# Two of the four blocks of a mixer's v by seven products of quarters

## The chip, the cores and the metric

The kernel runs on one core of a Trainium2 chip. The metric is the device time of one execution in microseconds (us). The median of three timed runs of the kernel before is 1301.42 us (1301.41 to 1302.15). The profile is one more execution, of 1302.33 us by its own time, with a span of 1300.6 us from the first to the last instruction. The engines are named as in the profile: PE multiplies matrices, PEld loads its weights, DVE and ACT work on whole tiles, POOL does a few small things and issues some transfers, and SP issues most transfers.

## The reference

The model is a trunk of two layers over 512 tokens of width 1024, in float32. The first layer mixes tokens with a gated MLP; the change is in the product that makes this mixer's `z`, and of that in the half `v` (columns 2048 to 4095 of `w_in`).

```python
h = rms_norm(x, norm_mix[0])            # x * rsqrt(mean(x*x) + EPS) * gain
z = gelu(h @ w_in)                      # w_in: 1024 x 4096
u, v = split(z, 2, axis=-1)             # 512 x 2048 each
v = rms_norm(v, v_gain)
sv = einsum("gts,bcsgd->bctgd", tril(w_s), v in chunks of 128 tokens) + b_s
x = x + (u * sv) @ w_out
```

A gated convolutional MLP, a recurrent mixer, another gated MLP and a final norm follow, and are not touched.

## The kernel before, in words

Every float32 factor is split in two parts in PE's reduced format: `hi` is the rounded value (an ACT copy), `lo` the rest (a DVE subtraction). A product is three matmuls: hi by hi, lo by hi, hi by lo.

The product for `v` is made in four blocks of 512 columns (`fb`, 0 to 3). In a block each of the four groups of 128 tokens (`c`) has one PSUM bank of its own, `pss[c]`, 128 x 512; there are eight banks in all (pool `pp`). The 1024 rows of the weight are loaded in four steps (`kc`) of two slices of 128. A step is two slices by four groups by three, 24 matmuls of 512 columns: the parts of x are the stationary operand, the parts of the weight the moving one. Block 0 also loads and splits x (`first_chunk`); after it `norm_stat` adds up the squares and POOL raises the mean to the power -0.5. The result `rc` (L222, one factor for each token) scales the product of every block on its way through gelu: `v_gelu`'s two ACT instructions (L382 and L385 before, L446 and L449 after) read a bank, write `vr`, square it and leave the sum in `vsum`. After the last block the sums give a second factor `rv`, and `vh` and `vl` (L395 and L396, after L520 and L521) are the parts of the normed v.

Then come the four blocks of `u`, where x moves and the weight is stationary. Their result has the tokens along the free axis, so the factor `rc` must be spread over the partitions: `norm_spread` builds two diagonal tiles `dg` on DVE (L238), multiplies them by ones on PE (L242, bank `rb`) and copies the bank to `rbc` on ACT (L243).

In the later MLPs the down projection is done by `seven` and `weight_sums` (L469 to L479 and L518): four quarter products of a 2 x 2 arrangement are replaced by seven products of sums of quarters, each with a bank of 128 x 2 x 256. One step of it is seven products by two halves by three, 42 matmuls of 256 columns. Its weights come by three SP transfers, and two sums of quarters are made on the way by a POOL transfer that adds to what lies in the tile (L471 before, L346 after).

The pool `wp` has three buffers for each of the tags raw, hi and lo; `wk` has six work tiles in the mixer. A scheduler orders the instructions of each engine when the program is built, and that order is then fixed.

## Time and profile before

| what | value |
|---|---|
| median of three runs | 1301.42 us (1301.41 to 1302.15) |
| profiled execution, own time | 1302.33 us |
| its span | 1300.6 us |
| PE busy | 1290.2 us, 99% of the span |
| DVE busy | 933.9 us, 72% |
| ACT busy | 602.0 us, 46% |
| POOL busy | 54.3 us, 4% |
| PE's share of the chain that ended last | 92% |

A duration in a row is that of one instruction from start to end; instructions of one engine overlap a little, so the pace of a row of them is read from their starts. Times in rows count from the span's start. The `v` blocks run from 5.66 to 94.70 us, `u` from there.

### The profile page before, as it was taken

The numbers are of one execution on the slowest core, as the hardware profiler recorded it, in microseconds if no ns is written. First come the engines' busy times: TensorE is split into PE (matmuls) and PEld (weight loads), VectorE is DVE, ScalarE is ACT, GpSimd is POOL, SyncE is SP. The second block draws the span as 40 slices with busy tenths as digits, with TensorE's granted clock in tenths as the row PEclk, the third lists the DMA queues.
The fourth block names the chain that finished last, engine by engine and source line by source line (L and its number), as shares of the span: only waits on it lengthen the run. The fifth ranks groups of instructions, "written<-read, shape, count | busy, mean of one in ns | idle before, by whom it ended". The sixth has DMA issues, their size and how long they took to land.

```text
span 1300.6 us, 17029 instructions
## 1 busy us (share of the span) xinstructions
PE 1290.2 (99%) x6510; PEld 1100.3 (85%) x6510; DVE 933.9 (72%) x1336; ACT 602.0 (46%) x809; POOL 54.3 (4%) x56
## 2 busy tenths in 40 slices
PE   9999999999999999999999999999999999999997
PEld 7888888888888998888998888888888899888886
DVE  7227775446877887878997799954687788576734
ACT  6456332333444543445554679633344444343432
POOL 1000000000000120001200000000000011000000
PEclk9999999999999999999999999999999999999998
DMA  6333222233233574235753323233223357332221
GB/s 235 98 97 113 82 81 82 97 97 98 97 98 105 125 184 137 94 98 122 171 150 98 98 81 97 98 114 97 85 95 98 112 141 184 114 97 98 98 81 65
DMA packets 121105, 143.47 MB, mean 110 GB/s; under 512 B 7616, under 2 KB 95168, under 8 KB 121024
## 3 DMA queue, kind: packets, MB, share of 16 engines
q1 hardware_dynamic: 111088, 132.95, 32.3%
q0 software_dynamic: 9792, 9.44, 4.9%
q8 instruction: 51, 0.84, 0.3%
q14 instruction: 30, 0.25, 0.1%
q10 hardware_dynamic: 144, 0.00, 0.0%
HBM read 140.26 MB, written 2.10 MB: 109 GB/s over the span
## 4 chain that ended last, share of the span: by engine, by line
PE 92%; DVE 3%; DMA 2%; issue 1%; ACT 0%; DVEq 0%; SPq 0%; POOLq 0%; POOL 0%
PE f L112 12%; PE f L111 12%; PE f L113 12%; PE d061m L518 2%; PE d101m L518 2%; PE d001m L518 2%; PE d100m L518 2%; PE v L370 2%; PE u L111 2%; PE aop L111 2%; PE u L112 2%; PE v L372 2%; PE aop L112 2%; PE v L371 2%; PE u L113 2%; PE aop L113 2%
## 5 line engine op out<-in xcount | busy, mean ns | idle before, releaser
L454 DVE SCALAR_TENSOR_TENSOR cv<-up,vt,cv 128x511 f32<-128x511 f32 x192 | 135.7, 744 | 0.7
L541 DVE TENSOR_TENSOR up<-f,rbc 128x512 f32<-128x512 f32 x96 | 63.6, 686 | 31.7 <-PE f L113 30.2
L452 ACT ACTIVATE cv<-up,vt 128x512 f32<-128x512 f32 x96 | 70.7, 804 | 0.8 <-DVE up L541 0.8
L557 ACT ACTIVATE cv<-cv 128x512 f32<-128x512 f32 x48 | 30.4, 633 | 38.5 <-DVE cv L454 38.4
L498 DVE TENSOR_TENSOR y<-yr,y 128x1792 fp32r<-128x1792 f32 x18 | 36.5, 2026 | 13.7 <-ACT y L497 13.7
L497 ACT CAST y<-yr 128x1792 fp32r<-128x1792 f32 x18 | 30.6, 1698 | 15.0 <-DVE yr L495 14.5
L222 POOL TENSOR_TENSOR rc<-ms,mhalf 128x4 f32<-128x4 f32 (+1 forms) x6 | 5.5, 911 | 651.0 <-DVE ms L221 651.0
L430 DVE SCALAR_TENSOR_TENSOR sv<-sv,vt,bs 128x256 f32<-128x256 f32 x32 | 14.9, 477 | 16.4 <-PE sv L427 16.4
L207 ACT ACTIVATE xh<-xall,vt 128x512 fp32r<-128x512 f32 x24 | 17.1, 718 | 20.3 <-DVE xall L259 15.8
L216 ACT ACTIVATE sq<-xall 128x512 f32<-128x512 f32 (+1 forms) x37 | 21.5, 586 | 9.8 <-DVE xall L271 9.8
L559 DVE TENSOR_TENSOR yr<-cv 128x512 f32<-128x512 f32 x36 | 24.6, 687 | 1.7
L454 DVE SCALAR_TENSOR_TENSOR xb<-xr,vt,xb 128x511 f32<-128x511 f32 (+2 forms) x36 | 25.5, 744 | 0.2 <-ACT xb L452 0.2
L217 DVE TENSOR_TENSOR acc<-acc,sq 128x512 f32<-128x512 f32 (+1 forms) x37 | 23.7, 641 | 2.0 <-ACT sq L216 1.9
L208 DVE SCALAR_TENSOR_TENSOR xl<-xall,vt,xh 128x512 fp32r<-128x512 f32 x24 | 17.8, 746 | 3.4 <-ACT xh L207 3.2
L426 PE MATMUL sv<-ws,vh 128*128 128x256 f32 x64 | 15.4, 325 | 0.0
L432 DVE SCALAR_TENSOR_TENSOR sv<-sv,vt 128x256 f32<-128x256 f32 x32 | 15.0, 479 | 0.4
L563 ACT CAST y<-cv 128x512 fp32r<-128x512 f32 x12 | 7.3, 619 | 16.4 <-DVE cv L561 16.4
L427 PE MATMUL sv<-ws,vl 128*128 128x128 f32 x64 | 14.2, 222 | 0.0
L694 DVE TENSOR_TENSOR_SCAN hs<-riyh,sq 128x512 f32<-128x512 f32 x12 | 14.0, 1203 | 0.0
L86 ACT ACT_TABLE_LOAD x10 | 12.8, 1283 | 0.1
L493 DVE TENSOR_TENSOR yr<-yr 128x512 f32<-128x512 f32 x18 | 12.4, 691 | 0.6
L445 ACT ACTIVATE u<-u 128x512 f32<-128x512 f32 x16 | 9.3, 624 | 7.1 <-DVE u L444 7.1
(2631 smaller groups left out, 4477.2 us busy)
## 6 DMA issues: line engine op xcount, KB each, us to landing
xall<-xT SPq DMA_DIRECT2D x8, 256.0 KB, 5.1
outT<-o SPq DMA_DIRECT2D x8, 256.0 KB, 2.1
av00raw<-a_w_in SPq DMA_DIRECT2D x2, 256.0 KB, 3.8
av01raw<-a_w_in SPq DMA_DIRECT2D x2, 256.0 KB, 5.2
av02raw<-a_w_in SPq DMA_DIRECT2D x2, 256.0 KB, 5.6
av03raw<-a_w_in SPq DMA_DIRECT2D x2, 256.0 KB, 4.9
bs<-a_b_s SPq DMA_DIRECT2D x1, 512.0 KB, 5.8
av10r<-a_w_in SPq DMA_DIRECT2D x1, 512.0 KB, 6.0
```

Source lines behind the costliest of these rows:

```text
L111: nc.tensor.matmul(ps, wh, xh, start=first, stop=False)
L112: nc.tensor.matmul(ps, wh, xl, start=False, stop=False)
L113: nc.tensor.matmul(ps, wl, xh, start=False, stop=last)
L370: nc.tensor.matmul(pss[c], xh[kk][:, ts], hi[:, k, :], start=kk == 0, stop=False)
L371: nc.tensor.matmul(pss[c], xh[kk][:, ts], lo[:, k, :], start=False, stop=False)
L452: nc.scalar.activation(dst, src, AF.Identity, scale=col(wname, woff + last * wstep), bias=col(cname, coff))
L454: nc.vector.scalar_tensor_tensor(dst[:, i:], src[:, :S - i], col(wname, woff + (last - i) * wstep), dst[:, i:], op0=ALU.mult, op1=ALU.add)
L497: nc.scalar.copy(hi, raw[:, 0:7])
L498: nc.vector.tensor_tensor(lo, raw[:, 0:7], hi.bitcast(F32), op=ALU.subtract)
L518: nc.tensor.matmul(banks[b][:, j], wt[:, w, js], xt, start=first and j == 0 and m == 0, stop=last and j == 1 and m == 2, skip_group_check= ...
L541: nc.vector.tensor_tensor(upt, pss[2 * half + j], rbc, op=ALU.mult)
L557: nc.scalar.activation(ts[0], ts[0], AF.Gelu_apprx_tanh)
```

## The change

Blocks 0 and 1 of `v` stay as they are. Blocks 2 and 3 are computed by the seven products that the down projections use. The four quarters of the left factor are two slices of x (k) by two halves of the tokens (t); those of the right one are the two slices of the weight by two halves of the block's columns. The sums of quarters of x are made once, in the four steps of block 1 (`v_sums`: for each step two scaled copies on ACT, four subtractions or additions of 256 elements on DVE, and the split of two tiles, two ACT copies and two DVE subtractions). The sums of the weight are made in each step of blocks 2 and 3 by `weight_sums`. A block of this kind holds seven banks, and at its end ACT and DVE combine the seven banks to the four tiles `vr`, on which `v_gelu` then works in place.

`norm_spread` is moved from block 1 of `v` to the first block of `u`, behind its second step. The work pool has five tiles in place of six, and the sixth tile's room is the pool `sm` of `weight_sums`.

```diff
-    mixer = enter(("yp", 24), ("wk", 6), ("bs", 1))
+    mixer = enter(("yp", 24), ("sm", 1), ("wk", 5), ("bs", 1))
...
+    def v_sums(q):
+        g = []
+        for k in (2 * q, 2 * q + 1):
+            t = work(f"xg{k}")
+            nc.scalar.activation(t, xs[k], AF.Copy, scale=g0[:, k:k + 1])
+            g.append((t[:, 0:HS], t[:, HS:S]))
+        (p_, q_), (r_, s_) = g
+        a, b = work(f"xa{q}"), work(f"xb{q}")
+        nc.vector.tensor_tensor(a[:, 0:HS], p_, q_, op=ALU.subtract)
+        nc.vector.tensor_tensor(a[:, HS:S], s_, q_, op=ALU.subtract)
+        nc.vector.tensor_tensor(b[:, 0:HS], a[:, 0:HS], s_, op=ALU.add)
+        nc.vector.tensor_tensor(b[:, HS:S], b[:, 0:HS], r_, op=ALU.subtract)
+        parts = [to_parts(t, f"xq{q}{i}") for i, t in enumerate((a, b))]
...
-    for fb in range(4):
+    for fb in range(2):
...
-            if fb == 1 and kc == 2:
-                norm_spread()
...
+            else:
+                v_sums(kc)
...
+    for fb in range(2, 4):
+        banks = seven_banks(f"v{fb}")
+        for q in range(KD // 2):
+            parts = weight_sums(wv4[:, 2 * q:2 * q + 2, fb], f"av{fb}{q}")
+            for b, part, w, i in PRODUCTS:
+                wh, wl = (t[:, w] for t in parts[part])
+                sh, sl = xsums[q][i]
+                for j in range(2):
+                    js = slice(j * P, (j + 1) * P)
+                    for n, (st, mv) in enumerate(((sh, wh), (sl, wh), (sh, wl))):
+                        nc.tensor.matmul(banks[b][:, j], st[:, js], mv, start=q == 0 and j == 0 and n == 0,
+                                         stop=q == KD // 2 - 1 and j == 1 and n == 2, skip_group_check=True)
...
+            nc.scalar.copy(e1, banks[1])
+            for j in range(2):
+                nc.vector.tensor_tensor(vraw[j, fb][:, n1], banks[2][:, j], e1[:, j], op=ALU.add)
+            nc.vector.tensor_tensor(u2, banks[6], e1, op=ALU.subtract)
+            nc.vector.tensor_tensor(u3, u2, banks[7], op=ALU.subtract)
+            for j in range(2):
+                nc.vector.tensor_tensor(vraw[j, fb][:, n0], u3[:, j], banks[4][:, j], op=ALU.subtract)
+            nc.scalar.copy(e5, banks[5])
+            nc.vector.tensor_tensor(u2, e5, u2, op=ALU.subtract)
+            for j in range(2):
+                nc.vector.tensor_tensor(vraw[2 + j, fb][:, n1], banks[3][:, j], u2[:, j], op=ALU.add)
+        for j in range(2):
+            nc.vector.tensor_tensor(vraw[2 + j, fb][:, n0], u3[:, j], e5[:, j], op=ALU.subtract)
+        for c in range(NC):
+            v_gelu(c, fb, vraw[c, fb])
...
-        pss = block(KD, loader_of(a_w_in, mb * 512, f"au{mb}"), xparts, f"u{mb}", spatial_hooks(mb - 1) if mb else {})
+        pss = block(KD, loader_of(a_w_in, mb * 512, f"au{mb}"), xparts, f"u{mb}", spatial_hooks(mb - 1) if mb else {1: [norm_spread]})
```

The products in their order are 1, 2, 4, 6, 7, 5, 3: the first three read the part tiles `a` of the weight (quarters), the other four the tiles `b` (sums).

The scheduler puts the instructions of the engines in a new order. POOL first, at the end of block 0 of `v`. Before, the power that gives `rc` stands alone between the power of `log_sigmoid` (`lu`) and the masks of `w_s` (`wsm`):

```order
L186 TENSOR_TENSOR lu<-lu,nabs 128x12 [waits DVE_49,Pool_49]
L222 TENSOR_TENSOR rc<-ms,mhalf 128x4 [waits DVE_49]
L405 AFFINE_SELECT wsm<-wsr 128x256 [waits DMAHW7_49,Activation_49]
L405 AFFINE_SELECT wsm<-wsr 128x256 [waits Activation_49] x3
L222 TENSOR_TENSOR rv<-ms,mhalf 128x4 [waits DVE_49]
```

Now, at the same place (DMAHW7 and DMAHW0 are the landings of the first two transfers of `av20r`, the raw weights of block 2's first step):

```order
L186 TENSOR_TENSOR lu<-lu,nabs 128x12 [waits DVE_49,Pool_49]
L346 DMA av20r<-a_w_in 128x2x256 [waits DMAHW4_49,DMAHW2_49,DMAHW7_49,DMAHW0_49,DVE_49]
L222 TENSOR_TENSOR rc<-ms,mhalf 128x4 [waits DVE_49]
L346 DMA av21r<-a_w_in 128x2x256 [waits DMAHW5_49,DMAHW3_49,DMAHW6_49,DMAHW2_49,DVE_49]
L346 DMA av22r<-a_w_in 128x2x256 [waits DMAHW6_49,DMAHW5_49,DVE_49]
```

The adding transfer for block 2 stands ahead of the power, and waits for two transfers that SP issues when `av11l` has freed their buffer.

ACT next, from the last split of block 1 to block 1's gelu (`v0` to `v3` are the banks of block 1, `vr01` the gelu of the first of them). Before:

```order
L99 CAST av13h_448<-av13r_446 128x1024 [waits DMAHW6_49,DVE_49,PE_49]
L99 CAST av20h_498<-av20r_496 128x1024 [waits DMAHW7_49,DVE_49,PE_49]
L243 COPY rbc_88<-rb_414 128x512 [waits PE_49]
L99 CAST av21h_528<-av21r_526 128x1024 [waits DMAHW0_49,DVE_49,PE_49]
L382 ACTIVATE vr01_476<-v0_342,rc_127 128x512 [waits PE_49]
```

Now twenty instructions stand between `av13h` and that gelu: eight scaled copies `xg`, eight splits `xq`, and four splits of weights. These are the last of them and what follows:

```order
L353 CAST av20bhi_576<-av20r_564 128x512 [waits DMASW0_49,PE_49]
L353 CAST av20bhi_576<-av20s_569 128x512
L429 ACTIVATE xg7_525<-xall_70,g0_90 128x512
L249 CAST xq30h_533<-xa3_527 128x512 [waits DVE_49]
L249 CAST xq31h_537<-xb3_528 128x512 [waits DVE_49]
L353 CAST av21ahi_630<-av21r_624 128x768 [waits DMAHW3_49,DMAHW4_49,DMAHW2_49,PE_49]
L446 ACTIVATE vr01_541<-v0_345,rc_130 128x512
L446 ACTIVATE vr11_545<-v1_346,rc_130 128x512
L353 CAST av21bhi_636<-av21r_624 128x512 [waits DMASW1_49,PE_49]
L353 CAST av21bhi_636<-av21s_629 128x512
L449 ACTIVATE junk_543,vsum_137<-vr01_541 128x512 [waits Activation_49]
L449 ACTIVATE junk_547,vsum_137<-vr11_545 128x512 [waits Activation_49]
```

Behind them comes the gelu of `v2` and then that of `v3`. On PE the fifth, sixth and seventh product of block 2's first step write to the banks of `v0`, `v1` and `v2`, and each waits for ACT; the first eight matmuls of the second step stand between the sixth and the seventh product.

DVE last, in the first block of `u`, around the two diagonal tiles (`rch`, `rcl` are the parts of `rc`). Before, both are built in block 1:

```order
L233 CAST rch<-rc 128x4 [waits Pool_49]
L234 TENSOR_TENSOR rcl<-rc,rch 128x4 [waits DVE_49]
L100 TENSOR_TENSOR av12l<-av12r,av12h 128x1024 [waits DMAHW5_49,Activation_49]
L238 TENSOR_TENSOR dg<-ident,rch 128x512
L238 TENSOR_TENSOR dg<-ident,rcl 128x512 [waits DVE_49]
```

Now:

```order
L514 TENSOR_REDUCE vtot_1117<-vsum_137 128x4 [waits Activation_49]
L238 TENSOR_TENSOR dg_1275<-ident_122,rch_132 128x512 [waits DVE_49]
L221 TENSOR_SCALAR ms_131<-vtot_1117 128x4 [waits DVE_49]
L521 SCALAR_TENSOR_TENSOR vl00_1123<-vr00_329,rv_1118,vh00_1122 128x512 [waits Activation_49]
L521 SCALAR_TENSOR_TENSOR vl10_1127<-vr10_333,rv_1118,vh10_1126 128x512 [waits Activation_49]
L521 SCALAR_TENSOR_TENSOR vl20_1131<-vr20_337,rv_1118,vh20_1130 128x512 [waits Activation_49]
L521 SCALAR_TENSOR_TENSOR vl30_1135<-vr30_341,rv_1118,vh30_1134 128x512 [waits Activation_49]
L238 TENSOR_TENSOR dg_1278<-ident_122,rcl_133 128x512 [waits PE_49]
```

The first diagonal stands behind the sum of all squares of v, the second also behind the first four `vl`. On PE the first of the two matmuls of `rb` stands behind 48 matmuls of `u`, the second eight matmuls later.

## Rows read from the trace of the kernel before

**Rows 1.** The page: busy time (share of the span) x instructions, by engine.

```profile
PE 1290.2 (99%) x6510; PEld 1100.3 (85%) x6510; DVE 933.9 (72%) x1336; ACT 602.0 (46%) x809; POOL 54.3 (4%) x56
```

**Rows 2.** Stretches: length, each engine's busy time (instructions), PE clock, DMA share, GB/s.

```profile
28.00:50.00 22.00, 22.00 (x102) 18.29 (x101) 7.29 (x15) 12.07 (x23) 1.01 (x1) 1.00 0.35 105
```

**Rows 3.** Timeline, PE: start, duration, instruction, count; first of block 1, `rb`, first of `u`.

```profile
28.74 0.49 PE L370 MATMUL v<-av10h,xh 128*128 128x512 f32 x1
...
39.77 0.64 PE L242 MATMUL rb<-dg,ones 128*128 128x512 f32 x2
...
94.70 0.39 PE L111 MATMUL u<-xh,au00h 128*128 128x512 f32 x1
```

**Rows 4.** Tile d001m of a down projection: count, ns min/median/max, first and last start.

```profile
L518 PE MATMUL d001m<-y,d0010ahi x12: 283/283/284, 468.6 to 470.5; 128*128 128x256 f32 x12
...
L518 PE MATMUL d001m<-y,d0013ahi x12: 283/283/284, 483.7 to 485.6; 128*128 128x256 f32 x12
```

**Rows 5.** Timeline, all engines: the factor `rc` and what ACT does with it.

```profile
28.91 0.16 DVE L221 TENSOR_SCALAR ms<-st 128x4 f32<-128x4 f32 x1
...
29.16 1.01 POOL L222 TENSOR_TENSOR rc<-ms,mhalf 128x4 f32<-128x4 f32 x1 [6.48 <-DVE ms L221]
...
30.20 1.26 ACT L382 ACTIVATE vr<-v,rc 128x512 f32<-128x512 f32 x2 [1.02 <-POOL rc L222]
...
34.95 1.05 ACT L99 CAST av13h<-av13r 128x1024 fp32r<-128x1024 f32 x1
```

**Rows 6.** Timeline, SP's queue: the issue of av20r, of one transfer before.

```profile
27.79 0.37 SPq L106 DMA_DIRECT2D av20r<-a_w_in  x1
```

**Rows 7.** Tile d0000r, a first step's raw weights: issues, first reader, landing.

```profile
L469 SPq DMA_DIRECT2D d0000r<-f_w_down x2: 367/416/464, 412.7 to 413.2; - x2
L470 SPq DMA_DIRECT2D d0000r<-f_w_down x1: 459/459/459, 413.7 to 413.7; - x1
L471 POOL DMA_DIRECT2D d0000r<-f_w_down x1: 1364/1364/1364, 417.4 to 417.4; - x1
L484 DVE TENSOR_TENSOR d0000s<-d0000r x1: 427/427/427, 423.3 to 423.3; 128x256 f32<-128x256 f32 x1
...
DMA to landing us min/median/max: 2.7/3.4/5.9
```

**Rows 8.** Timeline, DVE: four of the five instructions of one `weight_sums`.

```profile
456.07 0.43 DVE L485 TENSOR_TENSOR d0004s<-d0004r,d0004s 128x256 f32<-128x256 f32 x1
456.42 0.95 DVE L479 TENSOR_TENSOR d0004alo<-d0004r,d0004ahi 128x768 fp32r<-128x768 f32 x1
457.28 0.69 DVE L479 TENSOR_TENSOR d0004blo<-d0004r,d0004bhi 128x512 fp32r<-128x512 f32 x1
457.89 0.69 DVE L479 TENSOR_TENSOR d0004blo<-d0004s,d0004bhi 128x512 fp32r<-128x512 f32 x1
```

**Rows 9.** Timeline, ACT: block 1's first gelu; splits of 768 and 512 elements.

```profile
47.30 0.69 ACT L382 ACTIVATE vr<-v,rc 128x512 f32<-128x512 f32 x1 [0.31 <-PE v L372]
...
445.41 0.82 ACT L478 CAST d0002ahi<-d0002r 128x768 fp32r<-128x768 f32 x1
446.13 0.62 ACT L478 CAST d0002bhi<-d0002r 128x512 fp32r<-128x512 f32 x1
```

**Rows 10.** Timeline: the end of v's sums, the factor `rv` and its first readers.

```profile
97.32 0.17 DVE L389 TENSOR_REDUCE vtot<-vsum 128x4 f32<-128x16 f32 x1
...
99.58 2.74 DVE L396 SCALAR_TENSOR_TENSOR vl<-vr,rv,vh 128x512 fp32r<-128x512 f32 x4 [1.88 <-ACT vh L395]
```

**Rows 11.** Stretches near the end, where PE runs dry.

```profile
1289.50:1290.00 0.50, 0.50 (x6) 0.49 (x5) 0.50 (x2) 0.06 (x1) 0.00 (x0) 1.00 0.00 0
...
1292.50:1293.00 0.50, 0.00 (x0) 0.00 (x0) 0.34 (x1) 0.00 (x0) 0.50 (x1) 1.00 0.97 340
...
1293.50:1294.00 0.50, 0.47 (x1) 0.47 (x2) 0.00 (x0) 0.00 (x0) 0.00 (x0) 0.50 0.45 162
```

**Rows 12.** Timeline, PE: the ten matmuls ahead of everything.

```profile
1.26 4.45 PE L163 MATMUL warm<-warm 128*128 128x512 bf16 x10 [1.26 <-DVE warm L160]
```

More of the change, by code (lines that the diff above doesn't have):

```diff
@@ L331, in project_out, with weight_sums, part, fill @@
         leave(1, dg)
+    HS = S // 2
+    PRODUCTS = ((1, 0, 0, 0), (2, 0, 2, 1), (4, 0, 1, 6), (6, 1, 2, 5), (7, 1, 0, 4), (5, 1, 1, 3), (3, 1, 3, 2))
+    def weight_sums(src, name):
+        raw = wp.tile([P, 5, 256], F32, tag="raw", name=f"{name}r")
+        for k, n, to in ((1, 0, raw[:, 1:5:3]), (0, 1, raw[:, 0:4:3])):
+            nc.sync.dma_start(to, src[:, k, n:n + 1].broadcast_to([P, 2, 256]))
+        nc.sync.dma_start(raw[:, 2], src[:, 1, 1])
+        nc.gpsimd.dma_start(raw[:, 3:5], src[:, 0, 0:1].broadcast_to([P, 2, 256]), accum_op=ALU.add)
+        sums = phase["sm"].tile([P, 2, 256], F32, tag="sm", name=f"{name}s")
+        def part(n, t):
+            return tuple(wp.tile([P, n, 256], F32R, tag=g, name=f"{name}{t}{g}", padded_shape=[P, 4, 256]) for g in ("hi", "lo"))
+        def fill(hi, lo, src):
+            nc.scalar.copy(hi, src)
+            nc.vector.tensor_tensor(lo, src, hi.bitcast(F32), op=ALU.subtract)
+        with tc.high_priority(HIGH):
+            ah, al = part(3, "a")
+            fill(ah, al, raw[:, 0:3])
+            nc.vector.tensor_tensor(sums[:, 0], raw[:, 0], raw[:, 4], op=ALU.add)
+            nc.vector.tensor_tensor(sums[:, 1], raw[:, 2], sums[:, 0], op=ALU.add)
+            bh, bl = part(4, "b")
+            fill(bh[:, 0:2], bl[:, 0:2], raw[:, 3:5])
+            fill(bh[:, 2:4], bl[:, 2:4], sums)
+        return (ah, al), (bh, bl)
@@ new lines, in input_sums, with places @@
+    def input_sums(raw, dst):
+        nc.vector.tensor_tensor(raw[:, 3:5], raw[:, 0:3:2], raw[:, 7:8].broadcast_to([P, 2, HS]), op=ALU.subtract)
+        nc.vector.tensor_tensor(raw[:, 5], raw[:, 3], raw[:, 2], op=ALU.add)
+        nc.vector.tensor_tensor(raw[:, 6], raw[:, 5], raw[:, 1], op=ALU.subtract)
+        hi, lo = dst[:, :, 0:HS], dst[:, :, HS:S]
+        nc.scalar.copy(hi, raw[:, 0:7])
+        nc.vector.tensor_tensor(lo, raw[:, 0:7], hi.bitcast(F32), op=ALU.subtract)
+    def places(raw):
+        return raw[:, 0:8:7], raw[:, 1:3]
@@ new lines, in halves, with seven_banks, seven @@
+    def halves(t):
+        return t.rearrange("p (h t) -> p h t", h=2)
+    def seven_banks(name):
+        return {p[0]: psum(f"{name}m{p[0]}").rearrange("p (j t) -> p j t", j=2) for p in PRODUCTS}
+    def seven(pairs, weight, name):
+        banks = seven_banks(name)
+        for n, (q, x) in enumerate(pairs):
+            parts = weight_sums(weight(q), f"{name}{q}")
+            first, last = n == 0, n == len(pairs) - 1
+            for b, part, w, i in PRODUCTS:
+                hi, lo = parts[part]
+                for j in range(2):
+                    js = slice(j * P, (j + 1) * P)
+                    for m, (wt, xt) in enumerate(((lo, x[:, i, 0:HS]), (hi, x[:, i, 0:HS]), (hi, x[:, i, HS:S]))):
+                        nc.tensor.matmul(banks[b][:, j], wt[:, w, js], xt, start=first and j == 0 and m == 0,
+                                         stop=last and j == 1 and m == 2, skip_group_check=True)
+        return banks
@@ L504, in halves @@
-    def halves(t):
-        return t.rearrange("p (h t) -> p h t", h=2)
-    def seven(pairs, weight, name):
-        banks = {p[0]: psum(f"{name}m{p[0]}").rearrange("p (j t) -> p j t", j=2) for p in PRODUCTS}
-        for n, (q, x) in enumerate(pairs):
-            parts = weight_sums(weight(q), f"{name}{q}")
-            first, last = n == 0, n == len(pairs) - 1
-            for b, part, w, i in PRODUCTS:
-                hi, lo = parts[part]
-                for j in range(2):
-                    js = slice(j * P, (j + 1) * P)
-                    for m, (wt, xt) in enumerate(((lo, x[:, i, 0:HS]), (hi, x[:, i, 0:HS]), (hi, x[:, i, HS:S]))):
-                        nc.tensor.matmul(banks[b][:, j], wt[:, w, js], xt, start=first and j == 0 and m == 0,
-                                         stop=last and j == 1 and m == 2, skip_group_check=True)
-        return banks
```

68 lines of the change are left out of this document (25 added, 43 removed).

## The prediction

> **What bounds the kernel now.** I read the page first: PE is busy for 99% of the span, DVE for 72%, ACT for 46% [rows 1]. Then the stretches: in block 1 of v PE works all 22 us while DVE needs 7.3 and ACT 12.1 [rows 2]. So PE's stream sets the time in this stage, and a change gains what it takes out of that stream and loses every wait that it brings in. Third came the timelines of PE, ACT, POOL and SP around the two places where an engine waits for a result of all tokens: the factor `rc` after block 0 [rows 5], and the sum of squares after v [rows 10]. The order of the changed program says what stands where; all times are from the trace.
>
> **PE's own work.** From the first matmul of block 1 to the first of u, 28.74 to 94.70 us, lie 12 steps of 24 matmuls and the two of `rb` [rows 3]: 65.96 us for 290, so 0.2274 us each and 5.46 for a step. A step of the seven products is 42 matmuls of 256 columns. The down projection shows it: its steps 0 to 3 start at 468.6 to 483.7 us [rows 4], 5.03 us each, 0.120 for a matmul. Eight steps gain 8 x 0.43 = 3.4 us. Not more than that, since a matmul of half the columns takes 53% of the time, not half.
>
> [...]
>
> `rb`'s two matmuls are moved within PE's stream and neither gained nor lost as work.
>
> **First wait: the banks of block 1.** Block 2 holds seven banks, and four are free when it starts. The fifth product writes to the bank of `v0`, so it waits for block 1's first gelu. Block 2 starts at 28.74 + 96 x 0.2274 = 50.57, and after four products, 24 x 0.120, the fifth is due at 53.45. Before, that gelu started at 47.30, 0.31 us after the product was ready [rows 9]. Now it stands behind 20 other ACT instructions, and all of them behind `rc`.
>
> `rc` itself comes later. The two transfers that the adding one waits for go out at 27.79, when `av11l` frees the buffer as before [rows 6], and one issue of 0.4 later, 28.2. In the down projection POOL started 3.7 us after the last of three such issues and 4.2 after the second [rows 7]; that gives 31.9 to 32.4, and I take 32.1. The adding transfer holds POOL for 1.36 [rows 7] and the power for 1.01 [rows 5]: ACT has `rc` at 34.5, where it had it at 30.2. Nothing in the trace before shows an operation of POOL queued behind such a transfer. [...]
>
> From `rc` to `av13h` ACT took 30.20 to 34.95 [rows 5] for gelu and squares of block 0: now 34.5 + 4.75 = 39.25, and the split is done at 40.3, `av13l` on DVE at 41.5. PE wants them at 28.74 + 72 x 0.2274 = 45.1, so this lateness costs nothing there. From here DVE is the slower of the two. Up to the last result that ACT's `xq31h` needs it has 18 instructions of 256 elements at 0.35, nine of 512 at 0.61 and one of 768 at 0.86 (paces from the starts in [rows 8]): 6.3 + 5.5 + 0.9 = 12.7, so 54.2. ACT then does `xq31h` (0.62), `av21ahi` (0.72) and the gelu (0.69) [rows 9]: 56.2. In between the two engines hand results to and fro, eight times from DVE to ACT and back; most is covered by other work, and I add 0.65 for the rest. The gelu ends at 56.85, and PE has stood for 3.4 us. Bounds: 1.9 (POOL starts at 31.4, nothing lost to and fro) and 5.0 (POOL starts at 33, 1.5 lost).
>
> **Second wait.** The fifth and sixth products and eight matmuls of the next step, 20 x 0.120, bring PE to 59.25 at the seventh product, which needs the gelu of `v2`. ACT has, from the start of the first gelu at 56.15: two gelus, two splits, two squares, and the gelu of `v2`, 0.63 to 0.69 each [rows 5, 9] with some 0.1 of overlap between one and the next: 7 x 0.66 less 6 x 0.1 is 4.0, so 60.2. That is 1.0 us more, between 0 and 1.5. The rest of block 2 is free of waits: ACT and DVE need some 3.6 us in a step of 5.03, as in the down projection, whose steps run on without a break [rows 4]. The change of banks from block 2 to block 3 is like the one ahead of that tile; I cost it at nothing, at most 0.5. The transfers, 7 x 128 KB in 5.03 us, are 182 GB/s, well under the 340 of a stretch near the end [rows 11].
>
> **Third wait: `rb`.** Before, the diagonals stood in DVE's queue right behind `rc`. Now both depend on v's last sum. Count from the start of u. Combining seven banks and the gelu of the first two tiles go by while PE does its first step; then `au03h` needs a buffer that PE frees at 5.46, is done at 6.5, and two squares of 0.63 follow: 7.8. From the sum to the fourth `vl` took 97.32 to 99.58 + 2.74 = 102.32 [rows 10], 5.0, and the first diagonal adds 0.6: 13.4. The second diagonal (0.68) ends at 14.1. PE comes to the second matmul of `rb` after 57 x 0.2274 = 12.95, and waits 1.2; between 0 and 2.5. Behind it on PE stands the rest of this block, behind it on DVE the `vl` that the next block's spatial products need. These end some 6 us later against u than before, at about 24; the masks' parts and the four products with `rbc` follow, to about 28, and PE comes to the first spatial product at about 29. So this costs nothing, with a slack of 1 us.
>
> **Sum.** -3.4 + 3.4 + 1.0 + 1.2 = +2.2 us. The profiled execution of before took 1302.33 by its own time, so its like would take 1304.5; the median of the runs is 0.91 lower, and for it I forecast 1303.6.
>
> **Rivals.**
> *PE's clock falls in the first wait.* [...] The first ten matmuls show the price: 4.45 us [rows 12], 0.445 each for 512 columns against 0.227. The 20 matmuls up to the second wait would take 4.8 in place of 2.4, which swallows that wait: +1.4, and a few more at half pace give +1.8: 1305.4. [...]
>
> *The power does not wait for the transfer*, or the transfers land sooner. Then `rc` is there at 30.2, the whole ACT chain is 4.3 us earlier, the gelu of `v0` ends at 52.6 and the first wait is gone. What is left is at most the second and the third: -3.4 + 1.0 + 1.2 = -1.2, 1300.2. Against it speaks the order, in which the power stands behind.
>
> *Not slower but faster: the waits are covered.* If the scheduler's order holds in time as it does in the down projection, PE never stops, and all of 3.4 us is gained: 1298.0. For it: PE has no wait in the down projection [rows 4], and ACT is half idle in block 1 [rows 2]. It decides where the fifth product comes: if the gelu of `v0` ends before 53.45 and the second diagonal before 12.95 us of u.
>
> **How the numbers follow.** A measurement of this kernel can tell about 0.2% from no change, 2.6 us: faster is below 1298.8, slower above 1304.0. My forecast has 0.56, spread by its bounds over 1301.5 to 1305.2 with four tenths of it above 1304.0; the fall of the clock 0.18, all above; the power that does not wait 0.12, nearly all within; covered waits 0.10, below. The last 0.04 I give to what I have not thought of. Slower: 0.22 + 0.18 + 0.02 = 0.42. Faster: 0.10 + 0.02 = 0.12. Same: 0.46. The range from 1299.8 to 1306.2 leaves out the covered waits, a part of the rival ahead of them, and the far end of a clock that stays low.
>
> **What would show it.** In the profile after: POOL's power for `rc` starting at about 33.5 behind the transfer of av20r; PE idle once for some 3.4 us near 53.5 until ACT's gelu of block 1, and for about 1 us near 59; PE idle for about 1 us 13 us into u until DVE's `dg`; steps of blocks 2 and 3 of 5.03 us; a granted clock of 1.00 throughout. I am wrong if PE shows no wait near 53, if the steps take longer than 5.1 us, if blocks 2 and 3 show waits for weights in their later steps, or if the spatial products of u's second block wait.

## The result, and the profile after

The changed kernel took 1308.18 us (median of 6 runs, 1305.90 to 1309.46) against 1301.41 for the kernel before (6 runs, 1300.34 to 1302.15): a ratio of 1.0052, 95% interval 1.0042 to 1.0062, slower by 6.8 us. The prediction was 1303.6 with a range to 1306.2, so the direction of the sum (+2.2) was right and its size was not.

The profiled run of the changed kernel was its fastest (1305.9, span 1304.2), and the profiled run of before was slower than its six timed ones (1302.33, span 1300.6). The two traces therefore explain 3.6 us. The rest lies in runs that take longer than the profiled one; three more profiles of the changed kernel are read below for it.

The page after, to be held against [rows 1]. PE is busy 2.2 us less in a span that is 3.6 longer:

```profile
PE 1288.0 (99%) x6654; PEld 1105.2 (85%) x6654; DVE 968.2 (74%) x1414; ACT 619.5 (48%) x845; POOL 64.8 (5%) x64
```

PE's timeline after (start, duration, instruction; in brackets the idle time ahead of it and what ended it). The first, second and fourth rows are the start of block 1, of block 2 and of u [rows 3]; the others are all waits of PE over 0.3 us between the start of v and the end of the second down projection:

```profile
28.30 0.49 PE L462 MATMUL v<-av10h,xh 128*128 128x512 f32 x1
...
50.20 0.28 PE L490 MATMUL v2m<-av20ahi,xh 128*128 128x256 f32 x1
...
56.69 0.58 PE L490 MATMUL v2m<-av20bhi,xq00h 128*128 128x256 f32 x1 [3.46 <-ACT vr L446]
...
95.58 0.40 PE L111 MATMUL u<-xh,au00h 128*128 128x512 f32 x1
...
109.99 0.50 PE L242 MATMUL rb<-dg,ones 128*128 128x512 f32 x1 [1.28 <-DVE dg L238]
...
618.24 0.39 PE L396 MATMUL d060m<-y,d0607blo 128*128 128x256 f32 x1 [0.77 <-DVE d0607blo L354]
...
637.35 0.39 PE L396 MATMUL d060m<-y,d06011alo 128*128 128x256 f32 x1 [0.86 <-DVE d06011alo L354]
```

Before, PE's waits for the parts of d00 and d06 (the weights of the two down projections of the first MLP, each for one half of its rows) were 0.36 and 0.37 us:

```profile
445.33 0.39 PE L518 MATMUL d000m<-y,d0001blo 128*128 128x256 f32 x1 [0.36 <-DVE d0001blo L479]
...
633.26 0.39 PE L518 MATMUL d060m<-y,d06011alo 128*128 128x256 f32 x1 [0.37 <-DVE d06011alo L479]
```

From such landmarks the 3.6 us are put together:

| stretch | before | after | difference |
|---|---|---|---|
| start of block 1 | 28.74 | 28.30 | -0.4 |
| block 1 to the start of u | 65.96 | 67.28 | +1.3 |
| u's start to its fourth step (`au03h`) | 16.32 | 18.41 | +2.1 |
| from there to the end of d06 (`d06011alo`) | 522.24 | 523.36 | +1.1 |
| end of the program (last `rb` pair 1.22, then 0.70) | | | -0.5 |

Ahead of the first wait stands what the prediction described: POOL's adding transfer, the power behind it, ACT's gelus behind that [rows 5 show the same before, with the power at 29.16]:

```profile
32.02 1.38 POOL L346 DMA_DIRECT2D av20r<-a_w_in  x1 [9.59 <-DMA av20r<-a_w_in]
32.93 1.55 POOL L222 TENSOR_TENSOR rc<-ms,mhalf 128x4 f32<-128x4 f32 x1
...
34.51 1.26 ACT L446 ACTIVATE vr<-v,rc 128x512 f32<-128x512 f32 x2 [5.78 <-POOL rc L222]
...
39.26 1.05 ACT L99 CAST av13h<-av13r 128x1024 fp32r<-128x1024 f32 x1
...
55.96 1.26 ACT L446 ACTIVATE vr<-v,rc 128x512 f32<-128x512 f32 x2
```

The stretches around the wait (length; busy time of PE, PEld, DVE, ACT, POOL; the granted clock; DMA share; GB/s) show what came instead of the second wait. PE stood from 53.2 to 56.7, and its granted clock went from 1.00 to 0.50 until about 59.8:

```profile
55.00:56.00 1.00, 0.00 (x0) 0.00 (x0) 0.65 (x1) 1.00 (x3) 0.36 (x1) 1.00 0.00 1
56.00:57.00 1.00, 0.31 (x1) 0.31 (x2) 0.96 (x2) 1.00 (x3) 0.84 (x1) 0.69 0.00 0
57.00:58.00 1.00, 1.00 (x6) 1.00 (x6) 0.29 (x2) 1.00 (x3) 0.00 (x0) 0.50 0.45 65
...
59.00:60.00 1.00, 1.00 (x7) 1.00 (x7) 0.90 (x3) 1.00 (x4) 0.00 (x0) 0.60 0.53 112
60.00:61.00 1.00, 1.00 (x10) 1.00 (x10) 0.00 (x0) 1.00 (x3) 0.00 (x0) 1.00 0.93 270
```

The 20 matmuls from the fifth product to the seventh take 56.69 to 60.54, 3.85 us in place of 2.4, and the gelu of `v2` is done at 60.0, so nothing is left to wait for. Where the clock stayed up, in again, filler and pow_first below, PE did wait there, 0.5 to 0.9 us.

### The profile page after: what moved, and what is told of

Same layout as the page of the kernel before. It is cut to its first block, busy times and chain, and to the rows that moved or that the text cites. A ratio compares the mean times of both kernels' runs of the same rounds, so it can differ in the third digit from the quotient of the medians.

```text
span 1304.2 us, 17523 instructions
## 1 busy us (share of the span) xinstructions
PE 1288.0 (99%) x6654; PEld 1105.2 (85%) x6654; DVE 968.2 (74%) x1414; ACT 619.5 (48%) x845; POOL 64.8 (5%) x64
## 4 chain that ended last, share of the span: by engine, by line
PE 91%; DVE 4%; DMA 2%; issue 2%; ACT 1%; POOL 0%; SPq 0%; DVEq 0%; POOLq 0%; ACTq 0%
PE f L111 13%; PE f L113 13%; PE f L112 13%; PE d101m L396 2%; PE d061m L396 2%; PE d001m L396 2%; PE d100m L396 2%; PE d000m L396 2%; PE aop L111 2%; PE aop L112 2%; PE aop L113 2%; PE u L111 2%; PE u L113 2%; PE u L112 2%; PE bx L113 2%; PE bx L111 2%
## 5 line engine op out<-in xcount | busy, mean ns | idle before, releaser
L577 ACT ACTIVATE xb<-xr,vt 128x512 f32<-128x512 f32 x12 | 9.7, 814 | 6.4 <-DVE xr L688 6.4
```

Of the source, the lines that this page charges most:

```text
L577: nc.scalar.activation(dst, src, AF.Identity, scale=col(wname, woff + last * wstep), bias=col(cname, coff))
```

## The experiments

Times are medians; the ratio is to the kernel before, run on the same chip.

| run | edit to the changed kernel | us (range, runs) | ratio, 95% interval |
|---|---|---|---|
| again | none | 1308.10 (1306.29 to 1310.44, 5) | 1.0052, 1.0039 to 1.0065 |
| after_c, after_d | none | 1308.74, 1306.57 (one each) | |
| before_again | the kernel before | 1301.31 (one) | |
| pow_first | power ahead of av20r's transfer | 1305.01 (1304.30 to 1306.45, 5) | 1.0031, 1.0019 to 1.0043 |
| sums_late | last sum of x behind block 1's gelus | 1304.51 (1300.87 to 1307.56, 12) | 1.0023, 1.0015 to 1.0031 |
| filler | zeros multiplied during the first wait | 1304.65 (1304.43 to 1306.69, 5) | 1.0034, 1.0021 to 1.0046 |
| spread_back | spread as before, in block 1 | 1308.63 (1307.31 to 1308.81, 5) | 1.0053, 1.0041 to 1.0065 |
| spread_split | both `dg` made ahead of v's end | 1307.69 (1307.48 to 1309.37, 5) | 1.0053, 1.0041 to 1.0065 |
| combo | pow_first, sums_late, spread_split | 1302.40 (1299.43 to 1306.06, 12) | 1.0012, 1.0003 to 1.0021 |
| combo_b, combo_c | combo once more | 1303.35, 1301.62 (one each) | |
| combo_shift | combo, one fetch in two halves | 1302.34 (1299.42 to 1303.67, 11) | 1.0005, 0.9996 to 1.0013 |
| combo2 | combo, `rbc` copied sooner | 1301.17 (1299.57 to 1301.92, 11) | 0.9994, 0.9985 to 1.0003 |
| after_hold | fetch of d0607r held back | 1306.10 (1304.28 to 1307.39, 9) | 1.0029, 1.0020 to 1.0039 |
| combo2_hold | combo2 with that hold | 1299.34 (1298.68 to 1300.59, 11) | 0.9980, 0.9971 to 0.9989 |

### The first wait: pow_first and sums_late

pow_first queues POOL's adding transfer of av20r behind the power:

```
-        nc.gpsimd.dma_start(raw[:, 3:5], src[:, 0, 0:1].broadcast_to([P, 2, 256]), accum_op=ALU.add)
+        with tc.issue_after(power.pop()) if power else ExitStack():
+            nc.gpsimd.dma_start(raw[:, 3:5], src[:, 0, 0:1].broadcast_to([P, 2, 256]), accum_op=ALU.add)
...
-            norm_stat()
+            power.append(norm_stat().ins)
```

> The power that makes rc is queued on POOL ahead of av20r's adding transfer. If the prediction's first step is right, rc is ready at 29 to 30 us and not at 34.5, ACT's first gelu starts near 30.2, everything on ACT up to block 1's gelus is 3 to 4 us earlier, and the first wait shrinks from 3.46 to at most 0.5: with the clock 4 to 5 us faster than the changed kernel, about 1303.5. Rival: what paces ACT there is DVE's sums (ACT waits 0.9, 1.4 and 1.1 us for them), which start no earlier, and the wait stays over 2 us: 1306.5.

Measured: 3.1 us faster than the changed kernel (1308.1), where 4 to 5 was expected and 1.6 by the rival. Its timelines of POOL, DVE, ACT and PE:

```profile
29.48 1.01 POOL L222 TENSOR_TENSOR rc<-ms,mhalf 128x4 f32<-128x4 f32 x1 [6.70 <-DVE ms L221]
32.37 1.37 POOL L349 DMA_DIRECT2D av20r<-a_w_in  x1 [1.87 <-ACT vr L449]
...
38.49 0.43 DVE L362 TENSOR_TENSOR av20s<-av20r 128x256 f32<-128x256 f32 x1 [6.45 <-DMA av20r<-a_w_in]
...
54.92 1.26 ACT L449 ACTIVATE vr<-v,rc 128x512 f32<-128x512 f32 x2
...
55.65 0.39 PE L493 MATMUL v2m<-av20bhi,xq00h 128*128 128x256 f32 x1 [1.65 <-ACT vr L449]
...
59.07 0.39 PE L493 MATMUL v2m<-av20bhi,xh 128*128 128x256 f32 x1 [0.88 <-ACT vr L449]
```

`rc` is ready at 30.5 as expected, so the transfer was what held it. But the gelu moved from 55.96 only to 54.92: DVE has the sum of av20 ahead of block 1's last split and of all sums of x, and stands idle for 6.45 us until the same transfer has landed. The wait fell to 1.65, the clock stayed at 1.00 (the matmuls behind the wait start 0.12 apart), and the second wait of the prediction is there (0.88). So the rival's cause held, that DVE's sums pace ACT, but neither forecast of the wait did (at most 0.5, or over 2). With it falls what the prediction's own rival said of a power that doesn't wait: `rc` was 4 us earlier, and the gelu only 1.0.

sums_late leaves the power where it is and queues the last of the four sums on ACT behind block 1's gelus:

```
-            else:
+            elif kc < 3:
                 v_sums(kc)
...
-            v_gelu(c, fb, pss[c])
+            last_gelu = v_gelu(c, fb, pss[c])
+        if fb:
+            with tc.issue_after(last_gelu.ins):
+                v_sums(3)
```

> The last of the four sums of x is queued on ACT behind block 1's gelus, so those gelus go from 55.96 us to about 51, ahead of 53 us, when the fifth product is due. Theory W: the wait of 3.46 us and the stretch at half clock behind it (3.85 us for 20 matmuls that take 2.4) both go: 4.9 us faster than the changed kernel's profile, 1301.0, and the spread between runs is back to that of the kernel before (1.8 us): median 1301 to 1302. Theory F: the runs keep their spread and the median falls by 4.9 only, to 1303.3. Rival: the sums, now later, hold up step 3 of block 2 instead, and less than 2 us is gained.

Measured: 3.6 us faster than the changed kernel, the profiled run 1303.53 and 2.4 below that of the changed kernel. The first wait and the fall of the clock are gone (a first matmul behind a wait takes 0.39 here, as in pow_first, where it took 0.58 in the changed kernel with the clock down); in their place stand two short waits for parts that ACT, now busy with the gelus, splits later:

```profile
56.94 0.39 PE L494 MATMUL v2m<-av21alo,xh 128*128 128x256 f32 x1 [0.49 <-DVE av21alo L354]
...
59.73 0.39 PE L494 MATMUL v2m<-av21blo,xq11h 128*128 128x256 f32 x1 [0.30 <-DVE av21blo L354]
```

So both causes in the prediction's chain, a late `rc` and a gelu queued behind other ACT work, are real. Either remedy takes 3.1 to 3.6 us off, where I had expected 4 to 5 and 4.9 or more. The spread between runs did not shrink (6.7 us), against theory W.

### The clock: filler and the changed kernel again

filler adds 28 products with zeros to a bank that is already in use, between the fourth and the fifth product:

```
+                if fb == 2 and q == 0 and b == 7:
+                    for _ in range(28):
+                        nc.tensor.matmul(banks[1][0:64, 0], zero, parts[0][0][:, 0], start=False, stop=False,
+                                         skip_group_check=True)
```

> 28 matmuls of zeros, added to product 1's bank, stand between the fourth and the fifth product of block 2's first step, so that TensorE works through 28 x 0.12 = 3.4 us of the wait; nothing else changes. Theory C (the pause itself makes the clock fall): the granted clock stays 1.00 from 56 to 60 us and the 20 matmuls behind the wait take 2.4 us instead of 3.85, but then stand before the gelu of v2 for about 1 us: 0.5 us faster than the changed kernel, 1307.6, and the spread between runs gets no smaller. Rival: the clock falls there for another cause, and the time is as before or, with the fillers late in a run with a late start, 1 to 3 us longer.

The stretch and PE's wait in it:

```profile
57.00:58.00 1.00, 1.00 (x11) 1.00 (x10) 0.00 (x0) 1.00 (x3) 0.00 (x0) 1.00 0.65 80
```
```profile
58.84 0.39 PE L496 MATMUL v2m<-av20bhi,xh 128*128 128x256 f32 x1 [0.49 <-ACT vr L446]
```

With the same ACT chain and PE at work, the clock stays at 1.00 in each of the four stretches from 56 to 60, where it was 0.69, 0.50, 0.50 and 0.60; the pause made it fall. The second wait is back (0.49, predicted 1.0), and from the start of block 1 to u pass 66.75 us in place of 67.28, 0.5 less as expected. Even that is lost again in u, where the wait for `dg` is 2.01 in place of 1.28. So the profiled run (1304.61, 1.3 below that of the changed kernel) owes nothing of its gain to v and u: it lost 0.2 us to waits in the down projections where the changed kernel lost 1.6. The median is 3.5 us lower, where 0.5 was expected; how much of that is longer stretches at half clock that no longer occur is not shown.

The changed kernel three times more:

> The changed kernel once more, unaltered. Its profiled run (1305.9 us) was the fastest of six; the others took 0.8 to 3.6 us more. Theory W (waits and the clock fall behind the first): a second profile shows the fifth product of block 2 waiting 3.5 us again, and the matmuls behind it at half clock for a stretch of another length; a slower run has a longer stretch at half clock. Theory F (fetches far from the change, as the transfer into d0606r, whose issue took 1.42 us where 0.37 is usual, and cost 1.6 us): the stretch at 56 us is the same in every run, and a slower run has more waits of PE for DVE in the down projections.

> The changed kernel, unaltered, a third profile. Theory L (clock): a run near 1308 has a longer stretch at half clock behind the first wait than the 3.5 us of the profiled one. Theory M (start and down projections): the stretch is as long, and such a run loses more to waits for the parts of d00 and d06 (1.6 and 1.8 us so far) or starts block 1 later than 28.3 us.

(after_d had the same expectation.) The table is from PE's timeline and the stretches; the half-clock time is the sum over stretches of twice what the clock lacks to 1.00:

| run | us | block 1 starts | waits for block 1's gelus | at half clock, 56 to 64 us | block 1 to u | `au03h` to `d06011alo` | waits for d00, d06 |
|---|---|---|---|---|---|---|---|
| first profile | 1305.90 | 28.30 | 3.46 | 3.4 | 67.28 | 523.36 | 1.63 |
| after_d | 1306.57 | 28.62 | 3.56 | 3.4 | 67.53 | 523.43 | 1.65 |
| again | 1308.10 | 31.42 | 1.49, 0.77 | 0 | 64.97 | 524.05 | 1.83 |
| after_c | 1308.74 | 29.20 | 3.53 | 6.8 | 68.39 | 524.15 | 2.22 |

In after_c the clock is still down in the last but one of these stretches:

```profile
57.00:58.00 1.00, 0.34 (x1) 0.34 (x2) 0.96 (x2) 1.00 (x3) 0.59 (x1) 0.50 0.00 0
...
62.00:63.00 1.00, 1.00 (x7) 1.00 (x7) 0.00 (x0) 0.20 (x2) 0.00 (x0) 0.50 0.74 249
63.00:64.00 1.00, 1.00 (x10) 1.00 (x10) 0.00 (x0) 0.65 (x1) 0.37 (x1) 0.94 0.01 3
```

So the time at half clock behind the same wait differs between runs of one kernel: 3.4 us in two profiles, 6.8 in a third. In again PE's first matmul of v came 1.5 us later, the clock was at half in a part of block 0 (0.63 on the mean from 8 to 12 us), and block 1 began 3.1 us late; 2.3 of that was taken up by u's start, since ACT's chain moved less than PE. Against theory W its first wait was not 3.5 us but 1.49. Against the first profile, the span of after_c is 2.8 us longer: 0.9 by the start, 1.1 from block 1 to u, where the clock is down for longer, 0.1 in u, and 0.8 from `au03h` to `d06011alo`. That of again is 2.2 longer: +3.1 and -2.3 as told, +0.2 in u, +0.7 to `d06011alo` and +0.5 at the end of the program. So both theories, of the clock and of start and down projections, have their part in what these runs differ by.

### The spread of the scale: spread_back, spread_split, combo2

> The spread of the scale goes back into v's block 1, all else as changed. Theory W: the wait of 1.28 us for dg in u's first block goes, with 0.3 of restart; block 1 gets 0.63 us more on ACT and 1.4 on DVE, which can lengthen the first wait by up to 0.6: 1.0 to 1.6 us faster than the changed kernel (about 1306.9). Rival: the DVE work that held dg up is in the way of something else, and nothing is gained.

spread_back undoes this part of the change (`norm_spread()` after the third step of block 1). Nothing was gained, 1308.63, as the rival had it; but the reason was none that I had named:

```profile
47.11 0.69 DVE L238 TENSOR_TENSOR dg<-ident,rch 128x512 fp32r<-128x512 f32 x1
...
47.94 0.77 PE L242 MATMUL rb<-dg,ones 128*128 128x512 f32 x1 [4.54 <-ACT xg L429]
```

The `dg` now stands in DVE's queue behind sums of x and splits that keep DVE busy with hardly a gap from 40.31 to 47.11; PE waits 4.54 us in block 1, its clock falls there (0.84 on the mean from 32 to 52 us), and the later wait for the gelus is gone instead. That the scheduler put it so far back because it shares five work buffers with the sums of x is argued from the program and not shown; a place ahead of the sums was not tried.

spread_split makes both `dg` on DVE ahead of `vtot` and leaves the two matmuls in their place:

```
+    for part, to in ((rc, rch), (None, rcl)):
...
+        dg = work_r("dg")
+        nc.vector.tensor_tensor(
+            dg.rearrange("p (c t) -> p c t", c=NC), ident.unsqueeze(1).broadcast_to([P, NC, P]),
+            to.bitcast(F32).unsqueeze(2).broadcast_to([P, NC, P]), op=ALU.mult)
+        scales.append(dg)
+    def spread():
+        pb = psum("rb")
+        for i, dg in enumerate(scales):
+            nc.tensor.matmul(pb, ones, dg, start=i == 0, stop=i == 1)
+        nc.scalar.copy(rbc, pb)
     vtot = small(NC, "vtot")
...
-spatial_hooks(mb - 1) if mb else {1: [norm_spread]})
+spatial_hooks(mb - 1) if mb else {1: [spread]})
```

> DVE makes both dg of the scale's spread ahead of v's closing sums and products, and the two rb matmuls keep their place in u's first block. Theory W: the wait of 1.28 to 1.46 us for dg and the 0.3 us of restart behind it go, 1.6 us faster than the changed kernel: 1306.5. Rival: rv and with it v's parts come 0.7 us later on DVE and something behind them waits for that: 0 to 0.8 faster.

1307.69, 0.4 us below the changed kernel in place of 1.6: the wait for `dg` is gone, and another of the same size has come, so the rival's 0 to 0.8 holds, though at a place that it had not named. ACT copies `rb` to `rbc` behind all products of v, and u's second block needs a bank that only `rbc` sets free:

```profile
122.80 0.50 PE L111 MATMUL u<-xh,au10h 128*128 128x512 f32 x1 [1.25 <-ACT rbc L528]
```

combo joins pow_first, sums_late (with the gelus at high priority) and spread_split; combo2 adds a high priority for that copy (`with tc.high_priority(HIGH): nc.scalar.copy(rbc, pb)`).

> Three remedies together: the power ahead of av20r's transfer on POOL, the last sum of x behind block 1's gelus, both dg ahead of v's closing work. Theory W (the loss is these waits): no wait of TensorE over 0.3 us between 50 and 120 us; against the version with the sums alone (1304.5) another 0.8 us of waits for av21's parts and 1.6 for dg go: 1302. Theory P (place in the program): even so the two waits for d06's parts at 612 to 640 us stay, 1.2 to 1.6 us, since SP's slow issue at d0606r, which every profile of the changed order has and the one before has not, stays: 1302 and not below.

> The version with three remedies, and on ACT the copy of rb is queued ahead of v's remaining products: there it stood behind 16 of them, at 116.16 us, 14 us behind its matmuls, and u's second block waited 1.2 us for it with 0.3 of restart. Theory W: that wait goes too, 1.5 us faster than the version with three remedies, median 1300.9, best run near 1297.9, so that the median is at or just below that of the kernel before (1301.2). Rival: u's second block then waits for something else, and no more than 0.5 is gained.

Of the expectations for combo, theory W missed a wait, the one for `rbc`, and theory P missed too: SP's issue was slow at d0606r in combo's profile (1.8 us or more for the three issues, 1.35 before), and yet PE lost only 0.16 us to d06's parts. In combo blocks 2 and 3 run without a wait: block 2 starts at 50.73 and u at 91.04, 40.31 for eight steps. The wait for `rbc` is there (1.21 at 116.78) and is gone in combo2, where 0.47 for `u` on DVE remain at 119.08. The medians fall by 1.2 from combo to combo2 (by 1.7 against the kernel before on each one's chip), where 1.5 was expected. combo2 equals the kernel before, as expected, and still its profiled run lost this:

```profile
613.13 0.39 PE L399 MATMUL d060m<-y,d0607blo 128*128 128x256 f32 x1 [0.77 <-DVE d0607blo L357]
...
633.34 0.38 PE L399 MATMUL d060m<-y,d06011alo 128*128 128x256 f32 x1 [1.96 <-DVE d06011alo L357]
```

### The fourth wait, 500 us later: combo_shift, two more of combo, before_again, and the hold

> As the one with three remedies, and in each of v's eight steps one fetch is issued in two halves: eight more issues on SP ahead of everything that follows, no byte more. Theory P: SP's slow issues (1.2 to 1.6 us where 0.4 is usual) stand at other tiles than d0606r, and the waits for d06's parts change with them: up to 1.2 us faster or slower than the one with three remedies. Rival (the delay belongs to that place of the work, not of the program): d0606r is as late as ever, and the two are equal within 0.3.

> The version with three remedies again, for the profile of another of its runs, which lay between 1299.4 and 1306.1 us (the kernel before: 1300.5 to 1303.0). Theory S (the start): a run above 1302 has v's first matmuls later than 5.9 us and a stretch at half clock before 12 us, and is as the profiled one (1299.4) from there on. Theory D (transfers): the start is the same, and TensorE waits for av's or d0's and d06's parts. Theory C: a pause somewhere else lets the clock fall.

> The kernel before once more, unaltered. Its profiled run took 1302.33 us, its 23 other runs 1300.5 to 1303.0 with a median of 1301.2. Theory S: its start is as late in some runs as in the second profile of the changed kernel (block 1 at 31.4 us and not 28.7), and such a run takes 2.5 us more. Theory D: block 1 starts at 28.7 again and runs differ by waits of TensorE for DVE in the down projections (0.36 and 0.37 us in the first profile).

(combo_c had the expectation of combo_b.) combo_shift equals combo, as its rival had it, and SP's issue at d0606r stayed slow (1.8 or more): eight more issues ahead of it did not move it. combo_b (1303.35) and combo_c (1301.62) start like combo's first run and differ from it by waits for d00 and d06, 2.61 and 1.65 us against 0.16. before_again (1301.31) started block 1 at 28.44 and lost 0.22. Theory D, then: what makes these three runs of combo differ are transfers in the down projections.

The same place in the changed kernel, first profile (timelines of SP's queue, POOL, DVE):

```profile
585.01 1.83 SPq L344 DMA_DIRECT2D d0606r<-f_w_down  x2
...
590.36 1.21 POOL L346 DMA_DIRECT2D d0606r<-f_w_down  x1 [103.61 <-DMA d0606r<-f_w_down]
...
590.49 0.88 SPq L344 DMA_DIRECT2D d0607r<-f_w_down  x2
...
596.18 0.43 DVE L359 TENSOR_TENSOR d0606s<-d0606r 128x256 f32<-128x256 f32 x1 [4.39 <-DMA d0606r<-f_w_down]
```

and in the kernel before:

```profile
582.65 0.88 SPq L469 DMA_DIRECT2D d0606r<-f_w_down  x2
...
587.17 1.19 POOL L471 DMA_DIRECT2D d0606r<-f_w_down  x1 [100.25 <-DMA d0606r<-f_w_down]
...
588.14 0.88 SPq L469 DMA_DIRECT2D d0607r<-f_w_down  x2
...
592.06 0.42 DVE L484 TENSOR_TENSOR d0606s<-d0606r 128x256 f32<-128x256 f32 x1 [2.62 <-DMA d0606r<-f_w_down]
```

Two issues on SP take 1.83 us in place of 0.88; the adding transfer goes out later, at the same moment as the next step's fetch, and lands 5.8 us after its issue in place of 4.9. DVE stands in its queue before that sum and is late for all that follows. The profiles, in the order of the distance between the two issues (the landing is read from the adding transfer's issue to the start of DVE's sum, which waits for it):

| profile | next fetch behind the adding transfer | issue to DVE's start | PE's waits for d00, d06 |
|---|---|---|---|
| again | -0.08 | 6.12 | 1.83 |
| after_c | -0.06 | 6.18 | 2.22 |
| spread_back | 0.02 | 6.16 | 3.34 |
| sums_late | 0.06 | 6.06 | 1.42 |
| first profile after | 0.13 | 5.82 | 1.63 |
| combo_c, combo_b | 0.17, 0.22 | 6.14, 6.00 | 1.65, 2.61 |
| combo2 | 0.40 | 5.95 | 3.12 |
| pow_first, spread_split | 0.55, 0.55 | 5.64, 5.68 | 1.04, 1.99 |
| after_d | 0.66 | 5.78 | 1.65 |
| combo, combo_shift | 0.93, 0.97 | 5.20, 5.17 | 0.16, 0.35 |
| before | 0.97 | 4.89 | 0.73 |
| filler, before_again | 1.16, 1.17 | 4.21, 4.57 | 0.18, 0.22 |

The test: a copy of three elements on DVE makes the fetch of d0607r wait until d0606r has landed.

```
+        if name == "d0607":
+            with tc.high_priority(HIGH):
+                nc.vector.tensor_copy(raw[:, 0:3, 0:1], made["d0606"][:, 2:5, 0:1])
```

> The changed kernel, and in the second down projection the fetch of d0607r is held back until d0606r's adding transfer has landed (a copy of three elements on DVE). In 9 of 12 profiles of the changed order that fetch starts less than 0.6 us behind the adding transfer, which then lands 5.6 to 6.2 us after its issue, and TensorE loses 1.0 to 3.3 us to waits for the parts of d0; in the two profiles of the kernel before and three others it starts 0.9 to 1.2 us behind, the landing takes 4.2 to 5.2 and the waits 0.2 to 0.7. Theory K (that collision): the landing takes under 4.9, the waits fall below 0.7, and the kernel is 1.0 to 1.5 us faster than the changed one, about 1307. Rival: SP's slow issue at d0606r alone makes it late, or d0607r is now the late one, and the time stays at 1308 or rises.

> All four remedies in v and u's first block, and the fetch of d0607r held back too. Theory K: the profiled run without the hold lost 3.1 us in the down projections; with it at most 0.7 are lost and runs lie closer together: median 1299.5 to 1300, 1.5 us below that of the version without (1301.2) and 1.3 to 2 below the kernel before. Rival: as for the changed kernel with the hold, 1301 or more.

after_hold, the same timelines:

```profile
590.08 1.20 POOL L352 DMA_DIRECT2D d0606r<-f_w_down  x1 [102.81 <-DMA d0606r<-f_w_down]
...
594.25 0.42 DVE L365 TENSOR_TENSOR d0606s<-d0606r 128x256 f32<-128x256 f32 x1 [1.96 <-DMA d0606r<-f_w_down]
...
594.82 0.88 SPq L350 DMA_DIRECT2D d0607r<-f_w_down  x2
```

The transfer lands in 4.2 us, PE has no wait left in these down projections, and the kernel is 2.0 us faster than the changed one (1306.10; 4.2 above the kernel before on its chip, in place of 6.8). In v it has the first wait (3.52); the granted clock over its profiled run is 0.996 on the mean, 0.994 to 0.997 in the runs of the changed kernel. In the profile of combo2_hold SP's third issue was slow and the adding transfer went out 5.0 us behind the first one, as late as in combo2, and still:

```profile
580.95 1.56 SPq L353 DMA_DIRECT2D d0606r<-f_w_down  x1
...
585.05 1.20 POOL L355 DMA_DIRECT2D d0606r<-f_w_down  x1 [102.43 <-DMA d0606r<-f_w_down]
...
589.11 0.42 DVE L368 TENSOR_TENSOR d0606s<-d0606r 128x256 f32<-128x256 f32 x1 [2.32 <-DMA d0606r<-f_w_down]
```

It landed in 4.1 us and PE did not wait. So the fetch that goes out beside the adding transfer was the cause of the fourth wait, and not SP's slow issue alone. What makes SP's issue slow at that step is open: the three issues of d0606r took 1.8 to 2.7 us together, in place of 1.35, in 14 of 16 profiles of the changed order (not in filler and combo2) and in neither of the two of before. Nor is it the only way into the collision: in combo2 SP was on time, and POOL went out 5.1 us after SP's first issue, where the kernel before has 4.5 (582.65 to 587.17).

combo2_hold keeps, from the start of u to the last stage, one wait of PE over 0.3 us:

```profile
119.31 0.36 PE L584 MATMUL sv<-ws,vh 128*128 128x256 f32 x1 [0.51 <-DVE u L602]
...
1288.26 0.38 PE L283 MATMUL st<-ones_f,sq 128*128 128x1 f32 x2 [0.97 <-ACT sq L273]
```

At 1299.34 us, runs within 1.9 us of each other, it is the fastest version: 2.5 us below the kernel before (ratio 0.9980, 0.9971 to 0.9989) and 8.8 below the changed one. From block 1 to u pass 62.40 us in place of 65.96: 3.2 is what the seven products have to give, and the two matmuls of `rb` now stand in u.

## Why the prediction was wrong

- *PE's own work, -3.4.* Right but for 0.2. In blocks 2 and 3 a step without a wait takes 5.04 us. Before, block 2 started at 51.17, so its eight steps took 43.53, 5.44 each; the 5.46 from [rows 3] holds a part of the slower `rb` pair. Eight steps gain 3.2.
- *First wait, +3.4.* Right in place, chain and size: 3.46, with the fifth product at 56.69 (56.85 forecast), `rc` for ACT at 34.51 (34.5), `av13h` at 39.26 (39.25). That POOL holds the power behind the transfer was my estimate from the order alone, and nothing in the trace before shows it. The runs do: the power stands at 32.93 behind the transfer's 32.02, and at 29.48 in pow_first, where the transfer is not ahead of it. What the prediction had not seen is that DVE waits for the same transfer, so that an earlier power alone moved the gelu by 1.0 us.
- *Second wait, +1.0.* Wrong in kind. It was not there, since the rival with the clock, given 0.18, took place as well: 1.45 more for 20 matmuls, which start 0.21 apart at a granted clock of 0.50 and 0.12 apart at 1.00. The ten matmuls of [rows 12], from which that rival has its price, do not show it: the trace before has a granted clock of 1.00 in each stretch from 1 to 6 us, beside them. With the clock up the second wait is real, 0.77 (again), 0.88 (pow_first) and 0.49 (filler). I gave the fall no more than that for the rows near the end [rows 11], where the clock was 1.00 up to 1293.0; there PE had short work in between (0.83 us from 1291.0 to 1292.5), and here it had none. In two of four profiles the stretch was 3.4 us, in one 6.8, in one nil.
- *Third wait, +1.2.* Right in place and cause (DVE's `dg` behind four `vl`): 1.28, and with the restart of PE's stream (starts at 108.31, 109.99 and 110.32, where they lie 0.23 apart without a wait) 2.1 less the 0.45 of the two matmuls that moved, 1.6.
- *The stages behind u: left out of the sum, so taken as nothing, was +1.1.* This step failed too. The down projections were read for their pace alone, though PE waits of 0.36 and 0.37 there were in the trace before. The adding transfer of one step, late and beside the next fetch, became 1.6 us of waits, 0.9 more than before had; after_hold shows the cause.
- *From the profiled run to the median, taken as -0.9, was +2.3.* This is the step that failed by most: of the 4.6 us between the forecast of 1303.6 and the median of 1308.2 it holds 3.2, and the sum up to the profiled run 1.4. I carried the distance between the profiled run and the median of before over to the changed kernel. But the kernel with a wait that lets the clock fall, and with transfers that collide, has runs that differ more: 1305.9 to 1310.4 over 13 runs, against 1300.3 to 1304.4 over all runs of before. That its first profile was the fastest of them, and that of before a slow one, was chance. In again and after_c, which lie around the median, the 2.2 and 2.8 us more are what the table above shows: the late start in both, the longer stretch at half clock in after_c, and the down projections in both. As to before: before_again, 1.0 us below its first profile, took 1.0 less from `au03h` to the end of d06 and as long in v. Of the 6.8 us, 3.6 are in the first pair of profiles and 3.2 in this step (2.3 for the changed kernel, 0.9 for before).

In the terms of the sum: -3.2 + 3.6 (the fifth product comes 3.6 us after it was due) + 1.45 + 1.6 is +3.45, forecast +2.2; -0.4 for the start, +1.1 for the down projections and -0.5 for the end give the 3.6. That a sum of +2.2 came so near is in part luck: a wait that did not occur stood where the fall of the clock belonged, and the start and the end gave back 0.9 by chance.

What is shown: the first wait's two causes (pow_first, sums_late), that the pause lets the clock fall (filler, 1.00 in place of 0.50), the collision (after_hold, combo2_hold), and that with all these remedies the seven products gain (combo2_hold, 2.5 us below before). What stays open: how the 2.3 us of the median divide between longer stretches at half clock, late starts and the down projections. The shares are known for the three runs that have profiles, and not for the other nine; and why the start is late or the stretch long in one run and not in another, no run shows.

## What to carry to other kernels

Before a block takes more banks, follow what frees them through the queue of the engine that does it: a product that saves 0.4 us a step gains nothing if its fifth bank waits behind 20 instructions of ACT. When a wait is found, also read what stands next in each engine's queue, for three of the remedies here (pow_first, spread_back, spread_split) uncovered another wait, two of them as long as the first or longer. And a sum that is right for the changed stage still needs the margins of the later ones, and for the median more than one profile: one execution can be the fastest of all runs, as here, by 2 us.

## What was not expected of the hardware

- A transfer that adds to what lies in its tile took 4.1 to 4.6 us from issue to the first reader when the next fetch of 640 KB went out at least 1.16 us later (filler, before_again and the two with the hold), and 5.6 to 6.2 when it went out within 0.7 us.
- SP's three issues at one step took 1.8 to 2.7 us in place of 1.35 in 14 of 16 profiles of the changed order and its versions. They were on time in one profile of filler and one of combo2; whether their edits did that is not shown.
- In the same program the clock stayed at 0.50 for 3.4 us in two profiles (first, after_d) and 6.8 in a third (after_c), around a wait of PE of 3.5 us in each.
